# Banded attention divided behind the value product by transposed reciprocals, and a later place for some of VectorE's bit counts

## The chip, the cores and the metric

The kernel runs on one core of a Trainium2 chip. The metric is the device time of one execution in microseconds (us); lower is better. Engines are named as the profile names them: PE (TensorE, with PEld for its weight loads), DVE (VectorE), ACT (ScalarE), POOL (GpSimd), and SP, whose queue issues nearly all the DMAs.

## What is computed

The reference is one decoder block on 1024 tokens of width 1024. Two attention branches run side by side: a sparse one (branch a), in which an indexer scores all earlier keys and each query keeps its 256 best, and a banded one (branch b) with a window of 128 keys and a sink logit for each head. Each has 8 query heads and 2 key heads of width 64. Their outputs are gated, projected and added, and an MLP follows. The part that the change touches, cut:

```python
def swa_branch(q, k, v, sinks):                      # banded, branch b
    logits = einsum('bnqgrd,bnkgd->bngrqk', qb, kb) * HEAD_DIM ** -0.5
    logits = where(mask, logits, -inf)               # 0 <= t - s < 128
    p = softmax(concatenate([logits, sink], -1), -1)[..., :-1]
    return einsum('bngrqk,bnkgd->bnqgrd', p, vb)

def dsa_branch(q, k, v, q_idx, k_idx, w_idx, topk):  # sparse, branch a
    score = where(causal, einsum(relu(q_idx . k_idx), w_idx), -inf)
    _, sel = top_k(score, 256)                       # per query
    p = softmax(q . k[sel] * HEAD_DIM ** -0.5)       # not-yet-valid keys: -inf
    return p . v[sel]
```

## The kernel before

One launch goes through these stages, by the profile's clock: norm and first projections, indexer scores (up to about 240 us), the banded branch (240 to 440), the sparse branch (440 to 650), branch and output products (to 835), MLP up (to 1115) and MLP down (to the end). Float32 products run as three products of high and low halves.

**Steps and parts.** Each attention branch is a list of 16 steps, one for a pair (g, b): key head g with its four query heads, and query block b of 128 tokens. `pipeline` walks the list. The banded branch takes b = 0 to 7 for g = 0, then for g = 1; the sparse one takes the pairs in the order of `A_STEPS`, short ones first. In this text steps are numbered 0 to 15 (banded) and 16 to 31 (sparse). A step has two parts of two heads. A part's `scores` issues score products into a PSUM bank (L837), the masked minimum (L853, DVE), the exponential with its row sums (L856, ACT) and the reciprocals of the row sums (L860, DVE). The probabilities are then multiplied by the reciprocals: in the banded branch by L868 on DVE (`NORM` has 'd'), 128 x 256 for a head, in the sparse branch by L864 on POOL ('p'). `apply`, three parts later (`DEPTH` is 2), transposes the probabilities on PE (L879), splits them into halves (L104 on ACT, L109 on DVE, tile `of_w<-pt`), multiplies by the values (L884, L885, tile `pv`), and after the second part copies `pv` to SBUF (L892, ACT) and stores it.

**Bits.** The sparse branch's selection finds each query's 256th best score bit by bit. Query blocks 5 to 7 are counted on DVE: a bit is three counts (L676, 128 x 768, 896 and 1024) and some operations on 128 x 3 (L738, L739, and L737 on POOL), each bit waiting for the one before. Blocks 2 to 4 are counted on ACT (L678, with L741, L742 and L744 on DVE). `BITS` says how many DVE bits follow each banded step ('b') and precede each sparse step ('a'); there are 31 bits and a call that makes the thresholds. `select` (L776 to L782) then makes the mask of a block, on DVE and POOL.

**Filling work.** `fill` puts the gate products (tile `gt`, 128 x 512, 48 matmuls for a half gate) after steps, by `FILL`; the projections of later queries (tile `mm`) are spread likewise. The program is handed to a scheduler, which sets each engine's order from the program's order and its own timeline, so that an instruction may come well ahead of its place in the text. Each engine then runs its list strictly in order.

Of the kernel before, what the change touches and what calls it, by code (L numbers as in the profile page):

```python
# [16 lines left out]
ALU = mybir.AluOpType  # L17

P = 128
# [7 lines left out]
R = NH // NG  # L27
# [22 lines left out]
IB_BANK = ('tr', 'S', 'pt')  # L50
START = {'dve': 11, 'act': 11}
A_STEPS = [(0, 1), (0, 0), (0, 3), (0, 2), (1, 1), (1, 0), (1, 3), (1, 2), (1, 5), (1, 4), (1, 7), (1, 6), (0, 6), (0, 7), (0, 5), (0, 4)]
BITS = {'b': '2121212121212121', 'a': '1111112'}
ORDER = [(5, 0), (4, 0), (6, 0), (7, 0), (3, 0), (2, 0), (7, 1), (6, 1), (5, 1), (4, 1), (3, 1), (2, 1)]
GBUFS = 3
WBUFS = (2, 4)
# [11 lines left out]
EVAC = 'a'  # L68
# [26 lines left out]
def decoder_block(tc, I, out):  # L95
    nc = tc.nc
# [124 lines left out]
    ident = kept(P)  # L221
# [355 lines left out]
    for b in range(NB):  # L577
        ps = bank(IB_BANK[b % len(IB_BANK)], [P, 512], "mm")
        project(ps[:, :328], w, b)
        ik, st, sqk, ikr = (x() for x in small)  # L580
# [38 lines left out]
    u, o = {}, 0  # L619
# [47 lines left out]
    top, o = {}, 0  # L667
# [151 lines left out]
    def attention_parts(st):  # L819
# [9 lines left out]
        def scores(j0):  # L829
            if j0 == 0:  # L830
                st.mx, st.sm = att["mx"](), att["sm"]()
            both = bank("S", [P, 2, 2 * P], "S") if PAIR and N <= 2 * P else None

            def products(j, c, e):
                pS = both[:, j - j0] if both is not None else bank("S", [P, 512], "S")
                for a in range(2):
                    marks["S"] = nc.tensor.matmul(pS[:, :e - c], lhsT=st.unit(b, j), rhs=kT[:, a, k0 + c:k0 + e], start=a == 0, stop=a == 1).ins  # L837
                return pS

            if sink:  # L840
                with tc.issue_after(turned_i[0]):
                    nc.gpsimd.tensor_copy(st.both.rearrange("p (j n) -> p j n", j=2)[:, :, 0], sk[:, j0:j0 + 2])
            if both is not None:
                pS2 = [products(j, 0, N) for j in range(j0, j0 + 2)]
            for j in range(j0, j0 + 2):
                pe = st.both[:, (j - j0) * st.width:(j - j0 + 1) * st.width]
                p = pe[:, 1:] if sink else pe
                last = sk[:, j:j + 1] if sink else -MASKED
                for c in range(0, N, 512):
                    e = min(N, c + 512)  # L850
                    pS = pS2[j - j0] if both is not None else products(j, c, e)
                    init, last = last, st.mx[:, j, c // 512:c // 512 + 1]
                    nc.vector.tensor_tensor_reduce(out=p[:, c:e], in0=pS[:, :e - c], in1=st.bias(c, e), scale=-SCALE, scalar=init,  # L853
                                                   op0=ALU.add, op1=ALU.min, accum_out=last)
                pe = pe[:, :N + sink]
                nc.scalar.activation(pe, pe, AF.Exp, bias=last, scale=-1.0, accum_out=st.sm[:, j:j + 1])  # L856
                prob[j] = p
            on = NORM[st.name]
            inv = st.sm[:, j0:j0 + 2]
            nc.vector.reciprocal(inv, inv)  # L860
            for j in range(j0, j0 + 2):
                q, r = prob[j][:, :N], st.sm[:, j:j + 1]
                if on[j] == "p":
                    nc.gpsimd.tensor_scalar(q, q, r, 0.0, op0=ALU.mult, op1=ALU.add)  # L864
                elif on[j] == "a":
                    nc.scalar.activation(q, q, AF.Copy, scale=r)
                else:
                    nc.vector.tensor_scalar(q, q, r, None, op0=ALU.mult)  # L868

        def apply(j0):  # L870
            if j0 == 0:
                st.pv = bank("pv", [P, R, P], "pv")
            pv = st.pv[:, j0:j0 + 2]
            for a in range(0, n, 2):
                m = min(2, n - a)
                pt = bank("pt", [P, 2, 2, P], "pt")
                for k in range(m):
                    for j in range(2):
                        nc.tensor.transpose(pt[:, k, j], prob[j0 + j][:, (a + k) * P:(a + k + 1) * P], ident)  # L879
                ph, pl = att["ph"](), att["pl"]()  # L880
                split(ph[:, :m], pl[:, :m], pt[:, :m], "act")
                for k in range(m):
                    vs = v[:, kb0 + a + k].rearrange("p a d -> p (a d)")
                    nc.tensor.matmul(pv, lhsT=vs, rhs=ph[:, k], start=a + k == 0, stop=False)  # L884
                    st.last = nc.tensor.matmul(pv, lhsT=vs, rhs=pl[:, k], start=False, stop=a + k == n - 1).ins  # L885
            if j0 == 0:
                return

            o = att["o"]()
            marks["pv"] = st.last  # L890
            if EVAC == "a":
                nc.scalar.copy(o, st.pv)  # L892
            else:
                nc.vector.tensor_copy(o, st.pv)
            for x in range(2):
                stores.append(nc.sync.dma_start(st.dst[x, R * g:R * g + R, :, st.b * P:(st.b + 1) * P].rearrange("j d q -> d j q"), o[x * HD:(x + 1) * HD]).ins)
# [165 lines left out]
    for half in (1, 0):  # L1062
        for ft in range(KT):
# [12 lines left out]
            tr = bank("tr", [P, 4, P], "trx")  # L1076
# [351 lines left out]
```

## Time and profile before

| | us |
|---|---|
| median of 3 runs (lowest, highest) | 1456.59 (1454.28, 1456.62) |
| time of the profiled execution | 1455.47 |
| its span | 1453.7 |

| engine | busy us | share of the span |
|---|---|---|
| PE | 1374.5 | 95% |
| DVE | 1080.2 | 74% |
| ACT | 779.0 | 54% |
| POOL | 461.4 | 32% |

The shares are means over stages with different limits, and a busy PE is not PE at its peak. The change lies in the two attention branches, 410 of the 1453.7 us. So the rows further down are by stretch: A (240 to 380 us, banded steps 0 to 9), B (380 to 440, the other banded steps), C (440 to 510, sparse steps 16 to 20), D (510 to 560, steps 21 to 24) and E (560 to 650, the rest).

### The profile page before, as it was taken

The page shows a single profiled execution, that of the slowest core. Times are in us where ns is not written, and L with a number is a line of the kernel's source. Part 1 is how long each engine was busy: PE and PEld are TensorE (multiplying, and loading weights), DVE is VectorE, ACT ScalarE, POOL GpSimd, SP SyncE. Part 2 cuts the span into 40 slices and gives each one's busy share as a digit, 9 for nine tenths or more (in the row PEclk, how much of TensorE's full clock was granted, in tenths as well). Part 3 has the DMA queues.
Part 4 walks back from the last instruction along what each step waited for, and adds up shares of the span by engine and source line. Part 5 has one row for each costly group of instructions (what it writes and reads, how often), then busy time and mean ns, then how long its engine had stood idle before and what let it go on. Part 6 is the DMA issues. An engine that isn't in the chain of part 4 may idle for free.

```text
span 1453.7 us, 21243 instructions
## 1 busy us (share of the span) xinstructions
PE 1374.5 (95%) x7096; PEld 1163.6 (80%) x7096; DVE 1080.2 (74%) x2115; ACT 779.0 (54%) x1612; POOL 461.4 (32%) x455
## 2 busy tenths in 40 slices
PE   8999997888898899789999999999999999999998
PEld 6989886677797788677878778888888888888887
DVE  8667799999889988776753586566664788687674
ACT  6335445666783547654445476555554545445453
POOL 4373865663758773323515310000000000001001
PEclk9999998999999999899999999999999999999999
DMA  7321231322433221456456465344443978643323
GB/s 267 111 74 48 79 108 58 88 76 57 108 84 88 53 71 29 116 165 207 153 166 174 131 212 204 141 150 149 159 146 110 333 251 310 211 119 93 109 74 116
DMA packets 135822, 196.10 MB, mean 135 GB/s; under 512 B 16032, under 2 KB 59168, under 8 KB 135584
## 3 DMA queue, kind: packets, MB, share of 16 engines
q1 hardware_dynamic: 135568, 194.74, 42.6%
q8 instruction: 56, 0.92, 0.3%
q14 instruction: 54, 0.44, 0.1%
q10 hardware_dynamic: 144, 0.00, 0.0%
HBM read 132.03 MB, written 55.84 MB: 129 GB/s over the span
## 4 chain that ended last, share of the span: by engine, by line
PE 62%; DVE 21%; DMA 5%; ACT 4%; issue 4%; POOL 3%; SPq 1%; DVEq 0%; ACTq 0%; POOLq 0%
PE pu L1121 7%; PE pu L1123 7%; PE pu L1122 7%; DVE of_a L676 7%; PE pdx L1320 4%; PE pdx L1318 4%; PE pdx L1319 4%; PE pdy L1320 3%; PE pdy L1318 3%; PE pdy L1319 3%; DVE wide L853 2%; PE pso L113 2%; PE pso L115 2%; PE pso L114 2%; DMA uall<-z_d 2%
## 5 line engine op out<-in xcount | busy, mean ns | idle before, releaser
L1265 POOL TENSOR_TENSOR y<-x,gf 128x512 f32<-128x512 f32 x4 | 6.3, 1601 | 492.9 <-DVE x L1249 491.5
L104 ACT ACTIVATE dao<-da 128x512 fp32r<-128x512 f32 x112 | 70.0, 630 | 132.1 <-PE pdx L1320 52.5
L856 ACT ACTIVATE wide<-wide,of_a 128x257 f32<-128x257 f32 (+9 forms) x128 | 81.0, 634 | 80.4 <-DVE of_a L853 79.4
L113 PE MATMUL mm<-of_h,of_w 128*128 128x256 f32 x416 | 119.6, 288 | 0.5 <-ACT of_g L292 0.5
L114 PE MATMUL mm<-of_h,of_w 128*128 128x256 f32 x416 | 118.9, 287 | 0.0
L115 PE MATMUL mm<-of_h,of_w 128*128 128x256 f32 x416 | 118.7, 287 | 0.1
L676 DVE TENSOR_SCALAR_CACHE_REDUCE of_a<-wide,of_a 128x768 bf16<-128x768 bf16 (+5 forms) x93 | 106.1, 1141 | 1.0
L109 DVE TENSOR_TENSOR dao<-da,dao 128x512 fp32r<-128x512 f32 x112 | 76.4, 686 | 36.8 <-ACT dao L104 36.6
L1121 PE MATMUL pu<-XT,uo 128*128 128x512 f32 x256 | 99.8, 390 | 0.8 <-ACT snap L1154 0.8
L1122 PE MATMUL pu<-XT,uo 128*128 128x512 f32 x256 | 99.6, 389 | 0.0
L1123 PE MATMUL pu<-XT,uo 128*128 128x512 f32 x256 | 99.5, 389 | 0.0
L113 PE MATMUL gt<-of_h 128*128 128x512 f32 x224 | 91.4, 408 | 6.6 <-ACT of_h L335 6.6
L1319 PE MATMUL pdx<-dbo,dao 128*128 128x512 f32 x248 | 94.9, 389 | 0.0
L1318 PE MATMUL pdx<-dbo,dao 128*128 128x512 f32 x248 | 94.8, 390 | 0.0
L115 PE MATMUL gt<-of_h 128*128 128x512 f32 x224 | 91.0, 408 | 2.5 <-POOL of_h L109 2.5
L1320 PE MATMUL pdx<-dbo,dao 128*128 128x512 f32 x248 | 93.0, 390 | 0.0
L678 ACT ACTIVATE of_a<-uall,of_a 128x384 int8<-128x384 f32 (+2 forms) x93 | 66.8, 719 | 48.7 <-DVE of_a L744 28.5
L114 PE MATMUL gt<-of_h 128*128 128x512 f32 x224 | 90.8, 405 | 0.5 <-DVE of_h L336 0.5
L837 PE MATMUL S<-of_w 128*128 128x256 f32 (+3 forms) x320 | 79.4, 342 | 11.9 <-DVE of_a L853 11.9
L879 PE MATMUL pt<-kept,wide 128*128 128x128 f32 x408 | 72.7, 283 | 14.0 <-DVE of_a L739 6.3
L113 PEld LDWEIGHTS mm<-of_h,of_w 128*128 128x128 f32 x416 | 80.5, 194 | 1.6 <-ACT of_g L292 0.7
L115 PEld LDWEIGHTS mm<-of_h,of_w 128*128 128x128 f32 x416 | 80.1, 193 | 1.4 <-POOL of_w L109 0.5
(284 smaller groups left out, 4315.0 us busy)
## 6 DMA issues: line engine op xcount, KB each, us to landing
u_d<-u SPq DMA_DIRECT2D x112, 256.0 KB, 2.2
da<-u_d SPq DMA_DIRECT2D x112, 256.0 KB, 2.9
ur<-in_w_up_dram SPq DMA_DIRECT2D x32, 512.0 KB, 4.9
dr<-in_w_down_dram SPq DMA_DIRECT2D x64, 256.0 KB, 5.3
z_d<-of_g SPq DMA_DIRECT2D x32, 256.0 KB, 2.2
uall<-z_d SPq DMA_DIRECT2D x32, 256.0 KB, 3.4
raw<-in_w_out_dram SPq DMA_DIRECT2D x32, 256.0 KB, 4.2
of_g<-in_w_g_dram SPq DMA_DIRECT2D x28, 256.0 KB, 2.8
```

Source lines behind the costliest of these rows:

```text
L113: ins = nc.tensor.matmul(ps, lhsT=ah, rhs=bh, start=first, stop=False)
L114: nc.tensor.matmul(ps, lhsT=ah, rhs=bl, start=False, stop=False)
L115: nc.tensor.matmul(ps, lhsT=al, rhs=bh, start=False, stop=last)
L676: nc.vector.tensor_scalar(j, src, c, None, op0=ALU.is_lt, op1=ALU.add, accum_out=a)
L837: marks["S"] = nc.tensor.matmul(pS[:, :e - c], lhsT=st.unit(b, j), rhs=kT[:, a, k0 + c:k0 + e], start=a == 0, stop=a == 1).ins
L856: nc.scalar.activation(pe, pe, AF.Exp, bias=last, scale=-1.0, accum_out=st.sm[:, j:j + 1])
L1121: nc.tensor.matmul(ps, lhsT=ah, rhs=xh[:, at], start=f0, stop=False, skip_group_check=True)
L1122: nc.tensor.matmul(ps, lhsT=ah, rhs=xl[:, at], start=False, stop=False, skip_group_check=True)
L1123: nc.tensor.matmul(ps, lhsT=al, rhs=xh[:, at], start=False, stop=last, skip_group_check=True)
L1318: nc.tensor.matmul(ps, lhsT=ah[:, js], rhs=x[0][:, at], start=first, stop=False, skip_group_check=True)
L1319: nc.tensor.matmul(ps, lhsT=ah[:, js], rhs=x[1][:, at], start=False, stop=False, skip_group_check=True)
L1320: nc.tensor.matmul(ps, lhsT=al[:, js], rhs=x[0][:, at], start=False, stop=end, skip_group_check=True)
```

## The change

In the banded branch the probabilities are no longer multiplied by the reciprocals. After the value product of a step, its four columns of reciprocals are each spread over 128 columns and transposed on PE into one PSUM bank (`rb`, tag `tr`), so that row sums stand along the columns as in `pv`; ACT copies `pv` to SBUF as before, and DVE multiplies that copy by `rb` in place, ahead of the store. The sparse branch's own scaling on POOL stays. The second edit changes the table `BITS`: 20 instead of 24 calls after banded steps, and up to two ahead of each sparse step (calls past the thresholds do nothing).

```diff
-BITS = {'b': '2121212121212121', 'a': '1111112'}
+BITS = {'b': '1211121112111211', 'a': '2222222'}
...
             nc.vector.reciprocal(inv, inv)
-            for j in range(j0, j0 + 2):
+            for j in range(j0, j0 + 2) if st.name == "a" else ():
                 q, r = prob[j][:, :N], st.sm[:, j:j + 1]
...
             o = att["o"]()
             marks["pv"] = st.last
-            if EVAC == "a":
+            if st.name == "b":
+
+                rb = bank("tr", [P, R, P], "rb")
+                for j in range(R):
+                    nc.tensor.transpose(rb[:, j], st.sm[:, j:j + 1].to_broadcast([P, P]), ident)
+                nc.scalar.copy(o, st.pv)
+                nc.vector.tensor_tensor(o, o, rb, ALU.mult)
+            elif EVAC == "a":
                 nc.scalar.copy(o, st.pv)
```

In the changed file the transposes are L895, the copy L896 and the new product L897.

What the scheduler makes of it, at three places. First DVE in banded step 8, before:

```order
L860 RECIPROCAL of_a<-of_a 128x2
L676 TENSOR_SCALAR of_a<-wide,of_a 128x896
L744 TENSOR_SCALAR of_a<-of_a 128x3
L868 TENSOR_SCALAR wide<-wide,of_a 128x128 x2
L676 TENSOR_SCALAR of_a<-wide,of_a 128x1024
L738 TENSOR_TENSOR of_a<-of_a 128x3
```

and after (L741, L742 and L744 belong to ACT's bits):

```order
L741 TENSOR_TENSOR of_a<-of_a 128x3
L676 TENSOR_SCALAR of_a<-wide,of_a 128x1024
L742 SCALAR_TENSOR_TENSOR of_a<-of_a 128x3
L897 TENSOR_TENSOR of_a<-of_a,rb 128x512
L738 TENSOR_TENSOR of_a<-of_a 128x3
L744 TENSOR_SCALAR of_a<-of_a 128x3
L860 RECIPROCAL of_a<-of_a 128x2
```

The four L868 of a step are gone, and one L897 stands between the counts.

Second, DVE ahead of the 42nd pair of reciprocals, in sparse step 20. Before (L763 to L765 make the thresholds, L776 begins the mask of block 5):

```order
L738 TENSOR_TENSOR of_a<-of_a 128x3
L109 TENSOR_TENSOR of_w<-pt,of_w 128x256
L853 ISA wide,of_a<-S,of_a 128x256
L853 ISA of_a 128x1
L739 SCALAR_TENSOR_TENSOR of_a<-of_a 128x3
L763 TENSOR_SCALAR of_a<-of_a 128x3
L764 TENSOR_TENSOR of_a<-of_a 128x3
L853 ISA wide,of_a<-S,of_a 128x128
L853 ISA of_a 128x1
L765 TENSOR_TENSOR of_a<-of_a 128x3
L860 RECIPROCAL of_a<-of_a 128x2
L776 TENSOR_SCALAR of_a<-uall,of_a 128x768
```

and after:

```order
L441 TENSOR_TENSOR of_a<-of_a 128x512
L853 ISA wide,of_a<-S,of_a 128x256
L853 ISA of_a 128x1
L109 TENSOR_TENSOR of_w<-pt,of_w 128x256
L739 SCALAR_TENSOR_TENSOR of_a<-of_a 128x3
L676 TENSOR_SCALAR of_a<-wide,of_a 128x768
L853 ISA wide,of_a<-S,of_a 128x256
L853 ISA of_a 128x1
L676 TENSOR_SCALAR of_a<-wide,of_a 128x896
L860 RECIPROCAL of_a<-of_a 128x2
```

Where the thresholds stood, counts stand now. In all, 26 bits stood in the banded branch or ahead of it and 5 in the sparse one; now it is 24 and 7.

Third, PE near the end of sparse step 24, the first step of block 5. Before:

```order
L884 MATMUL pv<-of_w 128x256
L885 MATMUL pv<-of_w 128x256
L879 MATMUL pt<-kept,wide 128x128 x4
L884 MATMUL pv<-of_w 128x256
L837 MATMUL S<-of_w 128x512 x2
L885 MATMUL pv<-of_w 128x256
```

and after:

```order
L879 MATMUL pt<-kept,wide 128x128 x6
L884 MATMUL pv<-of_w 128x256
L115 MATMUL gt<-of_h 128x512
L113 MATMUL gt<-of_h 128x512
L114 MATMUL gt<-of_h 128x512
L115 MATMUL gt<-of_h 128x512
L837 MATMUL S<-of_w 128x512 x2
L885 MATMUL pv<-of_w 128x256
```

Gate products now stand among the last products of the step. Counted over the lists, with a step's end at its last value product, steps 0 to 9 hold 207 gate products before and 167 after, steps 10 to 16 24 and 26, steps 17 to 23 168 and 149, and steps 24 to 31 34 and 91.

## Rows read from the trace of the kernel before

**Rows 1.** Busy time by stretch; columns stand in its first line.

```profile
core 0: us, PE busy (x) PEld busy (x) DVE busy (x) ACT busy (x) POOL busy (x), PEclk, DMA share, GB/s
240.00:380.00 140.00, 115.51 (x691) 99.02 (x690) 135.62 (x399) 92.22 (x253) 74.74 (x112) 0.95 0.28 76
380.00:440.00 60.00, 55.62 (x428) 52.25 (x426) 49.18 (x144) 52.43 (x148) 38.78 (x46) 1.00 0.42 101
440.00:510.00 70.00, 61.48 (x380) 52.40 (x379) 68.36 (x160) 30.38 (x78) 54.51 (x54) 1.00 0.26 67
510.00:560.00 50.00, 50.00 (x291) 43.16 (x290) 40.17 (x84) 26.09 (x53) 32.01 (x25) 1.00 0.22 59
560.00:650.00 90.00, 77.82 (x470) 66.15 (x469) 72.27 (x173) 58.16 (x112) 30.77 (x27) 0.92 0.40 112
```

**Rows 2.** Chain that ended last, shares of the stretch by line: A, B, C, D.

```profile
by line: DVE of_a L676 41.0%; DVE wide L853 8.9%; DVE wide L868 8.7%; DVE of_w L109 6.2%; issue 5.5%; ACT of_a L678 3.4%; DVE of_a L741 3.0%; DVE wide L708 2.9%; DVE of_a L742 2.5%; DVE of_a L738 2.0%; DVE wide L709 2.0%; PE gt L113 1.7%; P
...
by line: issue 13.6%; ACT of_a L678 11.2%; ACT wide L856 8.9%; DVE wide L868 7.0%; DMA of_a<-of_a 6.7%; SPq L439 5.0%; DVE wide L853 4.7%; POOL of_a L441 4.6%; DVE of_a L742 4.3%; DVE of_a L744 4.1%; ACT of_a L436 3.1%; DVE of_w L109 3.1%; 
...
by line: DVE of_a L676 22.2%; issue 11.0%; DVE wide L853 9.2%; DVE of_w L109 6.3%; DVE of_a L738 4.2%; POOL of_w L456 3.7%; DVE uall L782 3.7%; POOL uall L777 3.6%; DVE of_a L441 3.6%; DVE of_a L781 3.5%; DVE uall L779 3.0%; DMA of_a<-of_a 
...
by line: PE gt L115 17.9%; PE gt L113 17.6%; PE gt L114 17.5%; PE S L837 15.0%; PE pt L879 13.1%; PE pv L885 7.9%; PE pv L884 7.6%; DVE wide L853 1.4%; ACT of_w L104 1.2%; DVE of_w L109 1.1%; issue 0.3%
```

**Rows 3.** Line L868 alone, by stretch, A and B: stretch, length, DVE busy, clock, DMA.

```profile
240.00:380.00 140.00, 17.49 (x43) 0.95 0.28 76
380.00:440.00 60.00, 12.88 (x22) 1.00 0.42 101
```

**Rows 4.** Instructions in order of time: start us, length us, engine, line, operation, count.

```profile
361.35 0.61 DVE L868 TENSOR_SCALAR wide<-wide,of_a 128x256 f32<-128x256 f32 x2
...
342.27 1.65 DVE L868 TENSOR_SCALAR wide<-wide,of_a 128x256 f32<-128x256 f32 x2
...
341.17 2.60 POOL L441 TENSOR_TENSOR of_a<-of_a 128x512 f32<-128x512 f32 x2
```

**Rows 5.** L109, L742 and L892 by line: count, then ns min/median/max, first and last start.

```profile
L109 DVE TENSOR_TENSOR of_w<-pt,of_w x112: 403/682/692, 250.9 to 646.4; 128x512 fp32r<-128x512 f32 x92, 128x256 fp32r<-128x256 f32 x20
...
L742 DVE SCALAR_TENSOR_TENSOR of_a<-of_a x31: 152/164/1245, 221.4 to 438.6; 128x3 int32<-128x3 int32 x31
...
L892 ACT COPY of_a<-pv x32: 563/574/595, 263.0 to 649.6; 128x512 f32<-128x512 f32 x32
```

**Rows 6.** Line L676 alone, by stretch, A and C.

```profile
240.00:380.00 140.00, 68.88 (x120) 0.95 0.28 76
...
440.00:510.00 70.00, 19.50 (x36) 1.00 0.26 67
```

**Rows 7.** DVE groups, 240 to 440 us: busy us, mean ns | idle before, releaser.

```profile
L738 DVE TENSOR_TENSOR of_a<-of_a 128x3 f32<-128x3 f32 x20 | 4.4, 222 | 0.0
...
L739 DVE SCALAR_TENSOR_TENSOR of_a<-of_a 128x3 f32<-128x3 f32 x11 | 1.7, 157 | 0.2
```

**Rows 8.** PE: a run of transposes on the chain, and gate products in order of time.

```profile
537.53 0.98 PE pt L879 x9
...
509.08 0.39 PE L115 MATMUL gt<-of_h 128*128 128x512 f32 x1
509.31 0.39 PE L113 MATMUL gt<-of_h 128*128 128x512 f32 x1
```

**Rows 9.** What DVE waited for in stretch A: us in total, times, longest.

```profile
DVE of_a L741 <- ACT of_a L678: 3.5, 2, 2.1
```

## The prediction

> **What bounds the kernel now.** The profile's page says that PE is busy 95% of the span and DVE 74%, a mean over stages. So I cut the two attention branches into five stretches and read busy time in each [rows 1], then the chain of work that ended last in each [rows 2], then the lines that the change touches, and last who waited.
>
> In stretch A, DVE is busy 135.62 of 140 us, and the chain is made of DVE lines: the counts 41.0%, the scaling L868 8.7%, which is 12.2 us [rows 1, 2]. What DVE waited for there is 3.5 us [rows 9]. A is bound by DVE. In B three engines stand close together, PE at 55.62, ACT at 52.43 and DVE at 49.18 of 60 us, and the chain passes from one to the other; L868 has 7.0% of it, 4.2 us [rows 1, 2]. In C DVE is busy 68.36 of 70 us and the counts lead the chain again. In D PE is busy for all 50.00 us and gate products alone hold 53% of the chain (17.9, 17.6 and 17.5), while DVE has 9.8 us free. In E no engine is full; PE has 12.2 us free [rows 1, 2]. So DVE's time is worth its length in A and C, about half in B, nothing in D; PE's time is worth its length in D.
>
> **The scaling, in A.** L868 costs 17.49 us of DVE there, in 43 instructions [rows 3]. Undisturbed, two of them take 0.61 us; with POOL at work, two took 1.65 us and ended as POOL's instruction did, 341.17 + 2.60 [rows 4]. At 0.305 us each the 43 would be 13.1 us, so 4.4 us of the 17.49 are stretch. The new product L897 reads SBUF and PSUM and writes 128 x 512. No row shows it; the nearest is L109 on `of_w<-pt`, the same size with one operand in PSUM, at a median of 682 ns and at most 692 [rows 5]. Ten steps cost 6.8 us. DVE gains 10.7 us if the stretch goes with L868, and 6.3 if it lands on the next instruction that can be held: the small L742 went from 152 to 1245 ns [rows 5]. I take 9.
>
> The row shows DVE held until POOL's instruction ends. The Trainium skill says so in "SBUF — State Buffer", section "SBUF: two separate sides": the port pair that the two engines share is locked for a whole instruction, and a DVE instruction takes part if it runs in a two-port mode or has two SBUF inputs. By that rule L897, with one SBUF input, is never held, which agrees with the maximum of 692 ns.
>
> **The bits, in A.** The table moves four calls; in the scheduler's order two bits move, from 26 and 5 to 24 and 7. A bit in A is 68.88 us / 20 = 3.44 us for its three counts and their accumulator reads (six instructions, 120 / 6 = 20 bits) [rows 6], and 0.222 + 0.157 for two small operations [rows 7]: 3.82, so 7.6 us for two. DVE loses 9 + 7.6 = 16.6 us in A. PE covers that: it gains 40 transposes at 0.98 / 9 = 0.109 us, 4.4 us, and loses 40 gate products at 0.23 us, 9.2 us [rows 8]. ACT has the same copies as before. I take the whole: **-16.6**, between -17 and -8 (with the wait of the third rival below).
>
> **The new waits.** The four transposes wait for DVE's reciprocals in PE's list. Before, the transposes of the probabilities waited for L868, which stood behind the same reciprocals, so no wait is longer. The reciprocals must now be kept until then; there are three sets for a pipeline three parts deep. Bank `tr` is otherwise free in these branches until their end. L897 is new behind ACT's copy (574 ns [rows 5]): while DVE stands at it, the counts and the next L853 are queued behind, and PE and ACT behind those. The store leaves later by L897's 0.68 us, and its reader comes only in E. I price this at nothing in the forecast, since the scheduler put counts between, and give it a rival.
>
> **Stretch B.** L868's 4.2 us leave the chain; its 12.88 us of DVE [rows 3] become six L897 at 0.68, 4.1 us. PE, nearly full, gets 24 transposes, 2.6 us. Bounds: -8.8 if DVE's saving counts, and +3 if PE's extra counts with two more gate products. I take **-3**.
>
> **Stretch C.** Two more bits. DVE counts there at 19.50 / 6 = 3.25 us a bit [rows 6], a little less than in A; I keep 3.82 with the small operations. DVE is full, and the masks of blocks 5 to 7 wait for the bits: **+7.6**, between +2 (if the free 9.8 us of D take them) and +7.6.
>
> **Stretches D and E.** The scheduler moved gate products later: steps 24 to 31 hold 91 instead of 34. 57 at 0.23 us are 13.1 us of PE, placed where PE has no free time in D and 12.2 us in E. Bounds 0 and +13.1. The row of D speaks for the full price, that of E for nothing; the added products stand in steps 24 and 25, across the border. I take **+6**.
>
> **Sum.** -16.6 - 3 + 7.6 + 6 = -6.0. The profiled execution took 1455.47 us (span 1453.7 and 1.8 around it), so 1449.5; the median of the runs, 1456.59, is 1.1 above the profiled one: **1450.6**. Its own range, with half the bounds at once, is 1443 to 1457.
>
> **First rival: the sparse branch takes back more than the banded gives.** The mechanism is the displaced gate products. In A they filled time in which PE waited for DVE and cost nothing; behind D they stand in a list that is full. Its price is all of 13.1 us there, and +3 in B, where step 16 now holds 24 of them and before none: -16.6 + 3 + 7.6 + 13.1 = +7.1, so 1463.7. It decides once gates and transposes cost 9.0 us together (16.6 - 7.6). For it: D's 50.00 of 50 and the 53% of gate products on the chain. Against it: DVE will be the later engine in C and D by two bits, and PE's wait for the masks is just what the scheduler fills.
>
> **Second rival: all is covered.** The gates go into E's 12.2 us and PE's waits for the masks, the bits into D's free DVE time: -16.6 - 4 + 2 + 0 = -18.6, so 1438. For it: two engines that are each full in only one of the two stretches. Against it: lists run in order, and no instruction moves up at run time.
>
> **Third rival: the swap gives DVE nothing.** L897 waits for the copy, which in ACT's list often stands behind exponentials and counts. At 0.9 us each in ten steps, about one and a half times the copy's 574 ns, the 9 us are gone, and the sum is -7.6 - 3 + 7.6 + 6 = +3, so 1459.6. For it: DVE has little slack and an ordered list. Against it: ACT is busy 92.22 of 140 us in A.
>
> A rule of the skill points the same way. "VectorE: DVE Perf Modes", section "The perf-mode tier table", has float32 tensor_scalar from SBUF at two elements a cycle, and tensor_tensor or any operand in PSUM at one. By the page's table of cycles a removed 128 x 256 would be an estimated 194 ns and L897 658 ns, so the 64 and 16 instructions would weigh 11.9 and 10.5 us, and the swap would save some 1.4 us in both branches. The rows have 30.4 us for the 64, undisturbed ones at 305 ns, so the measurement decides.
>
> **How the numbers follow.** Forecast 0.5, first rival 0.2, second 0.15, third 0.15. What can be told from no change is 0.2%, 2.9 us, so faster is below 1453.7 and slower above 1459.5. The forecast's own range puts 0.37 of its 0.5 on faster, 0.12 on the same and 0.01 on slower; the first rival 0.03 on the same and 0.17 on slower; the second 0.15 on faster; the third 0.03, 0.08 and 0.04. Sums: faster 0.55, same 0.23, slower 0.22. The range runs from the second rival's time to the first's, 1438 to 1463, and leaves out some 0.18 on both sides.
>
> **What would show it.** In the changed profile the copy of step 9 (the tenth L896; L892 before) should come some 17 us earlier; DVE should stay over 95% busy until then; L897 should be near 0.68 us each with no stretch, and the idle time ahead of it under 3 us in all. The first mask of block 5 (L776) should come some 12 us earlier than before, 20 from the banded branch less 7.6. Between it and the end of the sparse branch 6 us should be lost, with PE full and gate products on the chain up to step 25. The forecast is wrong in A if L742 and its like stretch by what L868 did, or if DVE waits ahead of L897; wrong behind it if the end of step 25 lies as far behind L776 as before, or 13 us further.

## The result, and the profile after

| | before | after |
|---|---|---|
| median us (lowest, highest; runs) | 1456.61 (1454.28, 1456.75; 4) | 1464.05 (1461.48, 1465.59; 4) |
| time of the profiled execution, its span | 1455.47, 1453.7 | 1461.48, 1459.5 |

The ratio is 1.0053 with an interval of [1.0037, 1.0068]: the change makes the kernel slower by half a per cent. The forecast had the wrong sign, and the time lies 1 us outside its range; it is within 0.4 us of the first rival's.

The rows from here on are those of the profiled executions, which lie 6.0 us apart where the medians lie 7.4. For the comparison the stretches are cut at ACT's copies of `pv`, so that both kernels have done the same steps at each cut: steps 0 to 9, 10 to 15, 16 and 17, 18 to 23, 24 and 25, 26 to 31. The kernel before:

```profile
core 0: us, PE busy (x) PEld busy (x) DVE busy (x) ACT busy (x) POOL busy (x), PEclk, DMA share, GB/s
240.00:380.20 140.20, 115.71 (x693) 99.22 (x692) 135.82 (x400) 92.42 (x255) 74.94 (x112) 0.95 0.28 76
380.20:434.90 54.70, 50.31 (x384) 47.03 (x384) 45.81 (x131) 47.44 (x135) 33.56 (x39) 1.00 0.41 99
434.90:445.80 10.90, 10.90 (x80) 10.20 (x80) 8.69 (x27) 7.20 (x19) 10.31 (x11) 1.00 0.55 121
445.80:537.60 91.80, 83.28 (x493) 70.89 (x492) 88.40 (x189) 38.87 (x96) 75.00 (x66) 1.00 0.23 62
537.60:562.60 25.00, 25.00 (x153) 21.06 (x151) 17.07 (x50) 17.03 (x34) 7.22 (x8) 1.00 0.18 49
562.60:649.60 87.00, 74.82 (x452) 64.16 (x452) 69.81 (x164) 55.92 (x109) 29.77 (x27) 0.92 0.41 115
```

and after, same steps, same columns:

```profile
240.00:371.50 131.50, 109.81 (x687) 96.86 (x686) 121.95 (x350) 91.32 (x251) 67.86 (x105) 0.95 0.27 73
371.50:419.90 48.40, 45.60 (x366) 43.22 (x364) 35.83 (x103) 43.80 (x121) 30.62 (x35) 1.00 0.44 111
419.90:442.00 22.10, 21.71 (x131) 19.03 (x132) 18.42 (x47) 12.05 (x34) 18.41 (x19) 1.00 0.35 87
442.00:532.30 90.30, 78.92 (x474) 66.83 (x474) 86.29 (x191) 39.17 (x95) 65.85 (x65) 1.00 0.24 62
532.30:568.30 36.00, 36.00 (x205) 30.80 (x204) 20.38 (x53) 17.82 (x36) 12.55 (x13) 1.00 0.17 52
568.30:655.70 87.40, 72.94 (x455) 60.34 (x454) 69.97 (x168) 56.68 (x108) 29.44 (x27) 0.98 0.39 115
```

By length: -8.7, -6.3, +11.2, -1.5, +11.0 and +0.4, +6.1 in all; what follows step 31 takes 804.1 and 803.8 us. The banded steps are 15 us shorter, and the next two steps and steps 24 and 25 give back 22.2. In those two places PE is busy for all or nearly all of the time (21.71 of 22.10, 36.00 of 36.00).

The gate products alone, by the same cuts, first before, then after (the second column is the length, then PE's busy time and the count):

```profile
240.00:380.20 140.20, 54.98 (x192) 35.85 (x192) 5.09 (x9) 0.95 0.28 76
380.20:434.90 54.70, 7.05 (x24) 4.12 (x24) 0.59 (x1) 1.00 0.41 99
434.90:445.80 10.90, 2.46 (x10) 1.81 (x10) 0.59 (x1) 1.00 0.55 121
...
537.60:562.60 25.00, 8.98 (x34) 6.10 (x34) 1.18 (x2) 1.00 0.18 49
```

```profile
240.00:371.50 131.50, 41.32 (x152) 26.72 (x152) 4.01 (x7) 0.95 0.27 73
371.50:419.90 48.40, 0.71 (x2) 0.30 (x2) 0.57 (x1) 1.00 0.44 111
419.90:442.00 22.10, 11.85 (x47) 8.54 (x48) 0.56 (x1) 1.00 0.35 87
...
532.30:568.30 36.00, 23.31 (x87) 15.35 (x87) 2.39 (x5) 1.00 0.17 52
```

The banded steps lost 62 products, at 0.23 us [rows 8] 14.3 us. Steps 16 and 17 got 37 more and steps 24 and 25 got 53 more, 20.7 us together, for 22.2 us of length; 27 of these 90 come not from the banded steps but from steps 18 to 23 (158 before, 131 after), which became only 1.5 us shorter. (The 0.23 us run from one product's start to the next. The busy times in the rows are higher, since they also count ends that overlap other work.) (A half gate is 24 such products, not 48 as the description of the kernel says.) The chain in steps 24 and 25 of after reads accordingly:

```profile
by line: PE gt L113 18.7%; PE gt L114 18.6%; PE gt L115 17.9%; PE S L837 11.6%; PE pt L879 10.7%; DVE wide L853 5.9%; PE pv L884 5.8%; PE pv L885 5.7%; POOL wide L864 3.2%; issue 3.1%; DVE of_w L109 0.7%; DVE of_a L860 0.5%; DVEq L109 0.1%;
```

More views of after. The transposes of reciprocals, with L897, in steps 0 to 9 and 10 to 15 (PE, PEld and DVE), and then four transposes in order of time with what follows them:

```profile
240.00:371.50 131.50, 7.91 (x40) 4.96 (x40) 6.11 (x9) 0.95 0.27 73
371.50:419.90 48.40, 4.48 (x24) 2.75 (x24) 4.09 (x6) 1.00 0.44 111
```

```profile
390.46 0.60 PE L895 MATMUL rb<-kept,of_a 128*128 128x128 f32 x4
390.90 0.60 PE L879 MATMUL pt<-kept,wide 128*128 128x128 f32 x4
```

The four are recorded as 0.60 us long, but the next product starts 0.44 us after the first, 0.11 us for each.

What DVE waited for in steps 0 to 9, which answers to [rows 9], and then L897 over the whole kernel, with its durations (ns, shortest, median, longest) and what DVE sat idle for ahead of it:

```profile
DVE of_a L860 <- ACT wide L856: 4.0, 3, 1.9
DVE of_a L741 <- ACT of_a L678: 2.7, 3, 1.5
DVE of_a L739 <- DVE of_a L742: 0.4, 1, 0.4
```

```profile
L897 DVE TENSOR_TENSOR of_a<-of_a,rb x16: 665/680/689, 261.9 to 422.2; 128x512 f32<-128x512 f32 x16
...
  ACT of_a L896: 0.3, 1
  DMA of_a<-of_a: 0.2, 1
```

Small operations of DVE in steps 0 to 9 (busy us, mean ns | idle before), first before, then after:

```profile
L741 DVE TENSOR_TENSOR of_a<-of_a 128x3 int32<-128x3 f32 x18 | 5.7, 315 | 3.5 <-ACT of_a L678 3.5
L742 DVE SCALAR_TENSOR_TENSOR of_a<-of_a 128x3 int32<-128x3 int32 x18 | 5.1, 283 | 0.0
L744 DVE TENSOR_SCALAR of_a<-of_a 128x3 int32<-128x3 int32 x18 | 4.3, 237 | 0.0
```

```profile
L738 DVE TENSOR_TENSOR of_a<-of_a 128x3 f32<-128x3 f32 x18 | 5.9, 326 | 0.1
L742 DVE SCALAR_TENSOR_TENSOR of_a<-of_a 128x3 int32<-128x3 int32 x17 | 5.7, 337 | 0.1
L741 DVE TENSOR_TENSOR of_a<-of_a 128x3 int32<-128x3 f32 x17 | 4.3, 253 | 2.7 <-ACT of_a L678 2.7
L744 DVE TENSOR_SCALAR of_a<-of_a 128x3 int32<-128x3 int32 x17 | 2.8, 164 | 0.1
L739 DVE SCALAR_TENSOR_TENSOR of_a<-of_a 128x3 f32<-128x3 f32 x9 | 2.4, 267 | 0.7 <-DVE of_a L742 0.4
```

### The profile page after: what moved, and what is told of

It reads as the page before. It is cut to its first block, busy times and chain, and to the rows that moved or that the text cites. A ratio compares the mean times of both kernels' runs of the same rounds, so it can differ in the third digit from the quotient of the medians.

```text
span 1459.5 us, 21272 instructions
## 1 busy us (share of the span) xinstructions
PE 1379.6 (95%) x7160; PEld 1168.3 (80%) x7160; DVE 1066.2 (73%) x2067; ACT 782.1 (54%) x1612; POOL 457.0 (31%) x455
## 3 DMA queue, kind: packets, MB, share of 16 engines
q1 hardware_dynamic: 135568, 194.74, 41.9%
## 4 chain that ended last, share of the span: by engine, by line
PE 65%; DVE 19%; DMA 4%; ACT 4%; issue 4%; POOL 2%; SPq 1%; DVEq 0%; ACTq 0%; POOLq 0%
PE pu L1130 7%; PE pu L1128 7%; PE pu L1129 7%; DVE of_a L676 6%; PE pdx L1327 4%; PE pdx L1325 4%; PE pdx L1326 4%; PE pdy L1327 3%; PE pdy L1325 3%; PE pdy L1326 3%; DVE wide L853 2%; PE pso L113 2%; PE pso L114 2%; PE pso L115 2%; PE gt L114 2%
## 5 line engine op out<-in xcount | busy, mean ns | idle before, releaser
L109 DVE TENSOR_TENSOR dao<-da,dao 128x512 fp32r<-128x512 f32 x112 | 76.4, 689 | 42.7 <-ACT dao L104 42.6
L676 DVE TENSOR_SCALAR_CACHE_REDUCE of_a<-wide,of_a 128x768 bf16<-128x768 bf16 (+5 forms) x93 | 106.2, 1142 | 1.2
L113 PEld LDWEIGHTS mm<-of_h,of_w 128*128 128x128 f32 x416 | 81.4, 196 | 1.3 <-DVE of_a L853 0.5
L114 PEld LDWEIGHTS mm<-of_h,of_w 128*128 128x128 f32 x416 | 81.5, 196 | 1.0
L115 PEld LDWEIGHTS mm<-of_h,of_w 128*128 128x128 f32 x416 | 81.2, 196 | 1.4 <-POOL of_w L109 0.5
```

The costliest lines, as they stand in the source:

```text
L113: ins = nc.tensor.matmul(ps, lhsT=ah, rhs=bh, start=first, stop=False)
L114: nc.tensor.matmul(ps, lhsT=ah, rhs=bl, start=False, stop=False)
L115: nc.tensor.matmul(ps, lhsT=al, rhs=bh, start=False, stop=last)
L676: nc.vector.tensor_scalar(j, src, c, None, op0=ALU.is_lt, op1=ALU.add, accum_out=a)
```

## The experiments

The theories. **Filling** (later: PE's account): the scheduler, finding less DVE work in the banded branch, puts less filling PE work there; it comes due where PE is full, at its full length. **Bits**: the two counts that moved cost more in the sparse branch than they bring. **New wait**: DVE's reciprocals now stop its list behind ACT's exponentials.

### One part of the change at a time

The swap alone has the changed file with `BITS` as before; the bits alone have the file before with the new table.

```diff
-BITS = {'b': '1211121112111211', 'a': '2222222'}
+BITS = {'b': '2121212121212121', 'a': '1111112'}
```

> The swap alone: division behind the value product by transposed reciprocals as in the changed kernel, the bits of both branches as in the kernel before. Three theories. Filling: the scheduler puts less filling TensorE work (gate products, 0.231 us each, and projections, 0.12 us) into the banded steps where VectorE has less to do; by the kernel's own order 93.8 us of it lie in steps 0 to 15 here, 104.9 in the kernel before and 89.5 in the changed one, so the loss stays for the most part although no bit has moved: 1458 to 1460 us, and steps 16 and 17 take some 18 us against 10.9 before. Bits: it is the two bits in the sparse branch that cost; without them the gain of the banded steps stands and the time is about 1447 us. New wait: VectorE's reciprocals and the bits behind them wait for ScalarE's exponentials in the banded steps, 5 us of new idle time, with the bits back in place: 1458 to 1464 us, with steps 16 and 17 as long as before.

Measured: 1469.63 us, ratio 1.0087 [1.0073, 1.0101], slower than the whole change. Some of that is not of this place: what follows step 31 takes 810.4 us against 804.1, and 4.4 us of it is one wait of PE in the MLP,

```profile
PE pdy L1325 <- ACT dao L104: 4.4, 1, 4.4
```

which no theory had. Up to step 31 the swap costs 7.8 us. Step 15 ends 5.6 us earlier than before, steps 16 and 17 take 28.3 us, steps 24 and 25 take 39.1 with 100 gate products (34 before):

```profile
429.30:457.60 28.30, 24.80 (x153) 21.69 (x153) 25.29 (x60) 14.25 (x40) 20.82 (x19) 0.98 0.25 59
...
534.00:573.00 39.00, 38.61 (x214) 32.90 (x213) 20.65 (x52) 18.07 (x36) 16.83 (x16) 1.00 0.16 48
```

So without any moved bit the loss is there, in the places that filling names; it doesn't need the bits. Nor does it need the reciprocals' wait, which is 0.3 us in steps 0 to 9 here (DVE's idle time there is 3.7 us more than before, ahead of other lines).

> The bits alone: the kernel before with the changed kernel's table of bits (two fewer 128x256 bits of VectorE in the banded steps 0 to 9, two more in the sparse steps), the division as before, with the broadcast multiply. Filling: the order keeps 103.4 us of filling TensorE work in steps 0 to 15 (104.9 before), so little is lost: about 1457 us, within 0.2% of the kernel before. Bits: what the sparse branch pays is here without the swap's gain: about 1463 us. New wait: no new wait is here, about 1457 us.

Measured: 1459.84 us, ratio 1.0021 [1.0008, 1.0035]: a small loss, between the two expectations. The banded steps gain 3.8 us, steps 24 and 25 lose 5.0 (51 gate products in place of 34, 3.9 us). Steps 16 and 17 become 8.0 us longer and steps 18 to 23 4.6 us shorter. Here it is projections (tile `mm`) that moved, 94 in steps 16 and 17 in place of 52, and DVE, too, is busy for 18.18 of the 18.90 us, so this run can't tell the bits' own price from that of the filling work.

### The displacement alone

```diff
+            n = 2 * self.ft + half
...
-                mm3(ps, wh, wl, h, l, kt == 0, kt == KT - 1)
+                with tc.issue_after(marks["hold"]) if n >= 21 and "hold" in marks else nullcontext():
+                    mm3(ps, wh, wl, h, l, kt == 0, kt == KT - 1)
```

`marks["hold"]` is the first sparse score product.

> The kernel before, with nothing of the change but its displacement of filling work: the gate halves from the 22nd on may be issued only behind the first sparse score product. By the order 154 gate products then stand in steps 0 to 9 and none in steps 10 to 15 (192 and 24 before; 152 and 2 in the changed kernel), and 90.5 us of filling TensorE work in all in steps 0 to 15 (104.9 and 89.5). Filling: the loss of the changed kernel appears without its gain, the banded steps end little earlier since they were not TensorE's: 1466 to 1470 us at the full price of the 14 us moved, 1460 at a half. Bits and new wait: nothing that they name is changed, about 1457 us.

Measured: 1474.51 us, ratio 1.0120 [1.0100, 1.0141], one of the two largest losses (the other is 1.0116 below), more than the full price. Rows of its steps 0 to 9 and 18 to 23:

```profile
240.00:382.00 142.00, 111.07 (x677) 95.84 (x676) 138.20 (x407) 93.22 (x256) 73.63 (x109) 0.93 0.28 74
...
457.40:554.50 97.10, 85.28 (x506) 73.42 (x505) 88.37 (x185) 39.76 (x97) 74.97 (x69) 0.98 0.24 63
```

Steps 0 to 9 don't get shorter with 36 fewer gate products in them (142.0 against 140.2 us): in the kernel before that work was free there. Steps 16 to 25 pay with 20.2 us (10.0, 5.3 and 4.9 by stretch), more than the 14 us that were moved. Up to step 25 PE's idle time rises by 15.6 us, about what was moved; the rest of the loss is mostly a lower clock (both in the table further down).

### The division left out

Seen from the changed file, with the table of bits of the kernel before:

```diff
-                rb = bank("tr", [P, R, P], "rb")
-                for j in range(R):
-                    nc.tensor.transpose(rb[:, j], st.sm[:, j:j + 1].to_broadcast([P, P]), ident)
                 nc.scalar.copy(o, st.pv)
-                nc.vector.tensor_tensor(o, o, rb, ALU.mult)
```

> Left out: the division of the banded branch, in either form (no multiply of the probabilities, no transposed reciprocals, no product behind). The bits are those of the kernel before. It is the bound of what any cheaper division can bring. By the prediction's own steps, in which VectorE's time is worth its length in steps 0 to 9 and half in 10 to 15, the 17.5 and the 4.2 us come back, less the 36 gate products, 8.3 us, that the order puts into steps 24 and 25 more than before: 1443 us, or 1435 were they free. TensorE's account (the runs so far: from step 0 to the end of step 25 TensorE's idle time is 37 us in the kernel before and 36 in the changed one, although VectorE lost 14 us of work in steps 0 to 9 alone; what moves the end of step 25 is TensorE's busy time): TensorE's work is that of the kernel before, so the end hardly moves: 1452 to 1458 us.

Measured: 1458.18 us, ratio 1.0011 [1.0001, 1.0021]. The prediction's own steps had given 1443 us; this is 0.2 us above the range of TensorE's account. With the whole division gone, 30.4 us of DVE by [rows 3], nothing is gained, although DVE's busy time in steps 0 to 15 falls by 22.3 us. Its six stretches:

```profile
240.00:375.60 135.60, 112.23 (x687) 96.14 (x686) 127.66 (x364) 92.72 (x255) 70.62 (x110) 0.96 0.27 73
375.60:425.20 49.60, 47.93 (x363) 45.07 (x362) 31.70 (x98) 43.69 (x123) 35.37 (x39) 1.00 0.45 114
425.20:443.80 18.60, 18.56 (x119) 16.33 (x118) 14.11 (x42) 12.74 (x36) 11.15 (x12) 1.00 0.36 86
443.80:534.50 90.70, 79.79 (x463) 70.20 (x463) 86.60 (x185) 38.56 (x94) 74.56 (x67) 0.92 0.24 62
534.50:569.40 34.90, 34.57 (x206) 30.03 (x205) 19.14 (x52) 19.62 (x39) 10.96 (x12) 1.00 0.16 46
569.40:652.00 82.60, 70.73 (x441) 60.35 (x440) 68.02 (x162) 54.72 (x105) 27.94 (x25) 0.96 0.41 122
```

Step 15 ends 9.7 us earlier. Steps 16 and 17 give 7.7 of that back, with 23 more gate products (5.3 us), and steps 24 and 25 another 9.9, with 36 more (8.3 us). Only 20 of these 59 products left the banded steps; steps 18 to 23 gave up 36 (122 in place of 158) and became only 1.1 us shorter. This is the shape of the changed kernel, without a new wait and without a moved bit. It bounds every cheaper division, as long as the filling goes where it went here.

### PE relieved

In both kernels one of the three products of the gates is left out:

```diff
-                mm3(ps, wh, wl, h, l, kt == 0, kt == KT - 1)
+                nc.tensor.matmul(ps, lhsT=wh, rhs=h, start=kt == 0, stop=False)
+                nc.tensor.matmul(ps, lhsT=wl, rhs=h, start=False, stop=kt == KT - 1)
```

> Left out: one of the three products of the gates' matmuls (high by low of the activations), a third of all gate products, in the kernel before. For the pair with the next run: by the order no gate product stands in steps 24 and 25 of either, and 33 and 112 in steps 18 to 23. TensorE has some 30 us less to do from 240 us on, so this one should be 15 to 30 us under the kernel before if TensorE's work counts there, and at most 8 us, what steps 24 and 25 held, if it is hidden behind VectorE.

> Left out: the same third of the gate products, in the changed kernel. TensorE's account and filling: with TensorE relieved the change does what VectorE's saving promises, at least 5 us less than the run before this one. Bits: what they cost in the sparse branch stays, 5 to 8 us more than the run before this one. New wait: nothing is gained in steps 0 to 9, 3 us more or less.

Measured: 1445.89 us (1444.91 to 1447.86) for the kernel before and 1438.03 us (1434.10 to 1439.84) for the changed one. Now the change is faster, by 7.9 us. Of the first run's two expectations neither came: it is 9.8 us under the kernel before as measured beside it (1455.66), far from the 15 to 30 of TensorE's account and just over the 8 of the other. The changed kernel gains some 25 us by the same relief (its ratio to the kernel before goes from 1.0053 to 0.9881). So before the change most of PE's relief brings nothing, and after it most of it counts. Steps 0 to 9 and 24 and 25, before and then after:

```profile
240.00:382.80 142.80, 119.15 (x697) 103.80 (x697) 140.56 (x391) 90.81 (x251) 75.93 (x114) 0.88 0.31 86
...
528.50:554.50 26.00, 19.72 (x110) 15.36 (x108) 24.21 (x57) 14.29 (x30) 13.59 (x10) 0.89 0.10 21
```

```profile
240.00:360.70 120.70, 104.56 (x685) 94.43 (x685) 117.53 (x332) 84.47 (x230) 71.40 (x110) 0.96 0.32 87
...
517.30:543.40 26.10, 20.08 (x118) 17.14 (x117) 26.04 (x59) 15.13 (x32) 11.56 (x9) 0.88 0.10 21
```

Steps 0 to 9 gain 22.1 us, and steps 24 and 25 lose nothing. Steps 16 to 23 take back 17.7 (89.6 and 107.3 us), since they hold two more bits and, by the order, 79 more gate products. With PE's load taken down the sign of the change turns; bits and new wait had forecast a loss or nothing. (The upper level of the clock is recorded as 0.95 in the first of the two, 1.00 in every other run; what follows step 31 takes 803.8 us in both, so its engines ran no slower there.)

### Attempts to keep the gain

Six versions of the changed kernel with another order or fewer transposes, each against a loss that its theory named.

```diff
-FILL = {'i': '000000000000', 'b': '0222011001010101', 'a': '1111011010101010'}
+FILL = {'i': '000000000111', 'b': '0332211010101010', 'a': '1100000000000000'}
...
+    with tc.issue_after(got[-1]) if got and (st.name, g, b) in AFTER else nullcontext():
```

(`got[-1]` is the gate half that `AFTER` names for the step whose score product this is.)

> The changed kernel, with the filling work held in the banded steps: another table of filling quotas, and the banded score products of steps 3 to 11 issued only behind a numbered gate half. By the order 221 gate products stand in steps 0 to 9, 29 in steps 10 to 15 and 51 in steps 16 and 17 (152, 2 and 46 in the changed kernel), and 101 us of filling TensorE work in steps 0 to 15 (89.5 there, 104.9 before). Filling: about 11 us of TensorE's work leave the full steps 16, 17, 24 and 25, and the banded steps cover it: about 1453 us. Bits and new wait: the cause is untouched, about 1464 us.

Measured: 1468.91 us, ratio 1.0081 [1.0066, 1.0095]; one of the six executions took 6436.8 us, which nothing here explains. Missed. Steps 24 and 25 fell to 20.5 us with 4 gate products, but steps 0 to 9 became 18.8 us longer than in the changed kernel for 17.6 us more of gate products (228 against 152). Forced ahead of score products, the filling costs its length there too: DVE then stands idle for 20.1 us in steps 0 to 9, and PE still for 24.9. Steps 16 and 17 take 47.9 us, steps 18 to 23 75.4.

```diff
-            inv = st.sm[:, j0:j0 + 2]
-            nc.vector.reciprocal(inv, inv)
+            if st.name == "a":
+                inv = st.sm[:, j0:j0 + 2]
+                nc.vector.reciprocal(inv, inv)
...
+                nc.vector.reciprocal(st.sm, st.sm)
                 rb = bank("tr", [P, R, P], "rb")
```

> The changed kernel with the banded branch's reciprocals taken at the end of a step, one 128x4 ahead of its transposes, in place of one 128x2 behind each part's exponentials: VectorE's list no longer stops behind ScalarE's exponentials. New wait: the 4.0 us that VectorE waited there in banded steps 0 to 9 go, 1459 us or better. Filling: by the order still fewer gate products stand in steps 0 to 9 (141, 192 before) and 84 in steps 24 and 25 and behind (91 in the changed kernel, 34 before), so 1462 to 1466 us. Bits: untouched, 1464 us.

Measured: 1471.16 us, ratio 1.0108 [1.0089, 1.0127], worse than both said. Step 9 ends 4.0 us earlier than in the changed kernel, and DVE waits 2.3 us for the exponentials where it waited 4.0. All of it and more is given back behind, in steps 18 to 23 (100.2 us) and 24 and 25 (37.4 us). So the wait was real, and taking a part of it away made step 9 end earlier but not the kernel faster.

```diff
-FILL = {'i': '000000000000', 'b': '0222011001010101', 'a': '1111011010101010'}
+FILL = {'i': '000000000000', 'b': '0222011001010101', 'a': '0000000000111111'}
```

> The changed kernel with another row of filling quotas for the sparse branch: none asked for by steps 16 to 25, the rest by steps 26 on, which lets the scheduler place them where its own timeline has room. The banded branch is as in the changed kernel (152 and 2 gate products in its two stretches), but 198 stand in steps 18 to 23 (127 there) and 53 in steps 24 and 25 (91 there, 34 before). Filling: 38 gate products of 0.231 us, 8.8 us, leave steps 24 and 25, where each cost its full length in the runs so far (12.2 us more of them made these steps 11 us longer in the changed kernel, 15.2 us 14 us longer in the swap alone), for steps in which TensorE waits for VectorE: 1455 us, 1459 if half of it is paid in steps 18 to 23. Bits and new wait: their causes are untouched, 1464 us.

Measured: 1461.17 us, ratio 1.0049 [1.0030, 1.0068], the same as the changed kernel. Steps 24 and 25 are 6.6 us shorter, steps 18 to 23 are 8.4 us longer, with 67 more gate products there. They don't hide behind DVE, which is busy 91.47 of 98.70 us. Part of it is the clock:

```profile
480.00:484.00 4.00, 2.32 (x15) 2.10 (x15) 4.00 (x11) 1.53 (x6) 3.74 (x6) 0.89 0.36 75
484.00:488.00 4.00, 2.91 (x12) 2.43 (x12) 3.96 (x14) 2.83 (x9) 1.52 (x4) 0.50 0.39 131
488.00:492.00 4.00, 4.00 (x15) 3.52 (x15) 3.94 (x15) 2.91 (x8) 3.04 (x5) 0.50 0.00 0
```

```diff
-            for j in range(j0, j0 + 2) if st.name == "a" else ():
+            for j in range(j0, j0 + 2) if st.name == "a" or g else ():
...
-            if st.name == "b":
+            if st.name == "b" and not g:
```

> The changed kernel with the swap in the first eight banded steps alone; steps 8 to 15 multiply the probabilities on VectorE as before, and the 32 transposes of reciprocals of these steps are gone (0.19 us each in the changed kernel). 160 and 35 gate products stand in the two stretches of the banded branch, 28 in steps 16 and 17, 55 in steps 24 and 25 (152, 2, 46 and 91 in the changed kernel; 192, 24, 10 and 34 before). Filling: 36 products, 8.3 us, leave steps 24 and 25, and 6 us of transposes leave the steps in which TensorE is the fullest: 1455 us. New wait: VectorE's waits lie in the first steps and stay, 1460 to 1464 us. Bits: 1464 us.

Measured: 1462.52 us, ratio 1.0056 [1.0037, 1.0074]. Missed. Steps 24 and 25 are 6.5 us shorter than in the changed kernel, as filling said, but steps 10 to 15 now take 59.8 us, more than in either kernel (48.4 and 54.7), with 42 gate products where the changed kernel has 2.

> Both of the last two: the swap in steps 0 to 7 alone, and the other row of quotas for the sparse branch. 160, 35, 18, 173 and 32 gate products stand in steps 0 to 9, 10 to 15, 16 and 17, 18 to 23, and from 24 on (152, 2, 46, 127 and 91 in the changed kernel; 192, 24, 10, 158 and 34 before). Filling: steps 24 and 25 hold no more than before, so what the swap and the bits gain in the banded steps is kept but for the bits' price in the sparse branch: 1450 us, 6 us under the kernel before. Bits: 1464 us. New wait: 1460 to 1464 us.

Both edits together. Measured: 1471.30 us, ratio 1.0116 [1.0098, 1.0135], far from the 1450 of filling. Steps 24 and 25 hold 32 gate products and take 27.9 us; but steps 10 to 15 take 60.1 us and steps 18 to 23 take 97.2 (48.4 and 90.3 in the changed kernel).

```diff
-                for j in range(R):
+                for j in range(2):
...
-                nc.vector.tensor_tensor(o, o, rb, ALU.mult)
+                nc.vector.tensor_tensor(o.rearrange("p (a b) d -> p a b d", a=2), o.rearrange("p (a b) d -> p a b d", a=2), rb[:, None].to_broadcast([P, 2, 2, P]), ALU.mult)
```

> Changed: the changed kernel with two transposes of reciprocals per banded step in place of four, so that heads 2 and 3 are divided by the row sums of heads 0 and 1. VectorE's product keeps its size. 32 transposes at 0.19 us, 6.2 us of TensorE, are gone; by the order 147, 7, 24, 200 and 40 gate products stand in steps 0 to 9, 10 to 15, 16 and 17, 18 to 23 and from 24 on (152, 2, 46, 127 and 91 in the changed kernel). TensorE's account: about 6 us less, 1458 us. Bits and new wait: as the changed kernel, 1464 us.

Measured: 1466.18 us, ratio 1.0069 [1.0057, 1.0081], no better than the changed kernel. Missed: steps 18 to 23 take 108.0 us with 200 gate products (131 in the changed kernel). (The 0.19 us for a transpose is busy time with its overlapping end; from start to next start a transpose takes 0.11 us, so the 32 left out free about 3 us and not 6.2. The same holds for the half swap.)

Behind step 31 the late reciprocals, the half swap, both edits and the two transposes lose another 2.6, 2.8, 5.6 and 5.1 us against the kernel before, which no theory names.

Filling had forecast 1450 to 1455 us for four of the six, and none came under the kernel before. So it says where the time of a given order goes; what another order will cost it didn't forecast.

### What the runs have in common

From step 0 to the end of step 25, PE's time is split here in three: busy time at full clock, busy time lost to a low clock (over slices of 2 us, busy time by one less the granted clock), and idle time. In the row "before, PE relieved" the level recorded as 0.95 counts as full.

| kernel | us to the end of step 25 | work | low clock | idle |
|---|---|---|---|---|
| before | 322.6 | 278.9 | 6.3 | 37.4 |
| after | 328.3 | 285.5 | 6.6 | 36.2 |
| swap alone | 333.0 | 282.3 | 13.4 | 37.3 |
| bits alone | 327.2 | 277.7 | 12.6 | 37.0 |
| no division | 329.4 | 282.4 | 10.6 | 36.3 |
| half and quotas | 337.5 | 284.4 | 14.1 | 39.0 |
| late reciprocals | 334.6 | 285.5 | 9.8 | 39.3 |
| two transposes | 334.4 | 282.6 | 14.4 | 37.4 |
| quotas | 328.7 | 282.1 | 13.8 | 32.8 |
| swap half | 333.0 | 280.9 | 11.0 | 41.1 |
| gates forced early | 340.2 | 285.0 | 11.7 | 43.6 |
| gates held back | 344.4 | 279.6 | 11.7 | 53.0 |
| before, PE relieved | 314.5 | 247.5 | 16.3 | 50.7 |
| after, PE relieved | 303.4 | 246.9 | 14.6 | 41.9 |

PE's idle time up to there is 36 to 39 us in eight of the twelve kernels with the full gates, whatever DVE has to do. In the changed kernel it fell by 1.2 us, while DVE's busy time fell by 24 us in steps 0 to 15 (181.6 to 157.8). So with the full gates, what the change did to the time up to step 25 is what it did to PE: 6.6 us more work, about what the 64 transposes hold PE for (6.0 us, from each one's start to the next product's). With PE relieved the change lowers the idle time by 8.8 us, from 50.7 to 41.9, and there DVE's saving shows. The same rows say which engine binds: in the kernel before, 31.4 us less work bring 8.1 us, since idle time and low clock take back 23.3; in the changed kernel 38.6 us less bring 24.9. The other orders also lose 3 to 8 us more to a low clock, which goes some way to say why none of them beats the kernel before: between steps 10 and 25 its clock is 1.00 in every stretch, as the rows above show, and so is that of after, while all ten others have dips there (0.92 in steps 18 to 23 of the run without division, 0.50 in the rows of the quota run).

## Why the prediction was wrong, step by step

**Stretch A.** Forecast -16.6, measured -8.7. DVE's busy time fell by 13.9 us (135.82 to 121.95). That is the lower end that the working gave, 6.3 + 7.6, in which the stretch that POOL gives lands on other instructions. In part it did: L738 went from 222 to 326 ns [rows 7], L739 from 157 to 267, L742 from a mean of 283 to 337. But L741 fell from 315 to 253 and L744 from 237 to 164; at their means before, the five lines would have taken 21.2 us and they took 23.8, so 2.6 of the 4.4 us show there. The bits were sized rightly (their counts fell from 68.88 to 62.05 us), and so was L897's 0.68 us. The longest L897 took 689 ns, so none was held by POOL, while L738, with two SBUF inputs, was (up to 1253 ns). The Trainium skill, "SBUF — State Buffer", section "SBUF: two separate sides", tells these two kinds of instructions apart in this way, and this trace agrees. The step that failed is "I price this at nothing": DVE's idle time rose by 5.2 us (4.4 to 9.6), 4.0 of it ahead of L860, behind ACT's exponentials.

**PE's part in A.** "PE covers that" held for A itself, and the transposes were priced rightly: from each one's start to the next product's, the 40 take 4.0 us (0.108 us in the median), against 4.4. The 7.91 us of busy time in the row above count each transpose's overlapping end too.

**Stretch B.** Forecast -3, measured -6.3, within its bounds. Only 2 gate products were left there, where 24 had stood; that lost cover reappears in steps 16 and 17.

**Stretch C.** Forecast +7.6. Steps 16 to 23 cost +9.7, but in another place: +11.2 in steps 16 and 17, where PE is full and got 37 more gate products, and -1.5 in steps 18 to 23, where the two bits lie and 27 gate products fewer. So the bits' own price isn't parted from the filling here. From step 17's end to the first L776 of block 5 it is 47.9 us against 43.3, which leaves them some 4.6, an estimate that puts all of the difference down to them. The view that the prediction named shows the sum: that L776 comes at 489.9 us against 489.0, not 12 us earlier. The working had priced displaced products behind step 23 alone; the 24 of step 16 stood only in the first rival.

**Stretches D and E.** Forecast +6, measured +11.4. The second step that failed is taking the displaced products at half their price. It is 5.4 us of the miss, beside 7.9 in A. It took both to turn the sign clearly: with this term alone put right the forecast's -6.0 would be -0.6, with A's alone +1.9. Steps 24 and 25 got 12.2 us more of gate products and became 11.0 us longer; the products fall due before E's free time comes.

**The sum.** Half the bounds at once give 1441.7 to 1461.5 us, not the 1443 to 1457 that the working states; the measured 1464.05 lies outside both.

**Why the first rival was right.** Its sum of +7.1 came out as +7.4 in the medians, and its mechanism, displaced filling at its full price, is what the runs show: the gates held back lose without the change, no division wins nothing, and with PE relieved the change wins. That the number fits so closely is luck, for its sizes were off against each other: A gave 8.7 and not 16.6, B gained 6.3 instead of losing 3, and the 9.7 of steps 16 to 23, for which it had the bits' 7.6, arose in steps 16 and 17 with 37 displaced products.

**What lay under it.** That DVE's time is worth its length in A, where it is busy 97%, was argued from A by itself. PE had 24.5 us idle there, and the scheduler used that room for work that is due later. When DVE's list got shorter the room did too (21.7 us), and a gain in A became a debt in D. The third rival, that the swap gives DVE nothing, had the wrong place: L897 waited 0.3 us for the copy, and DVE waited ahead of L860.

What stays open: the swap's 7.8 us up to step 31, the bits' 3.2 and the 6.1 of both don't add up, since each edit brings another order, and the experiments can't part an edit from its order. Whether some order holds 192 gate products in the shorter steps 0 to 9 at less than their length isn't known; the one that forced them there didn't. All eleven other kernels with the full gates have a higher median than the kernel before, even the bits alone, in which the division is untouched. So it isn't excluded that a part of each loss, and of the change's, is only that another order suits these steps less than the one before.

## What to carry to other kernels

Where a scheduler fills one engine's idle time in a stage that another engine binds, don't price that stage alone: follow the filling work to where it falls due, and charge it there at full length if that place is full. Add up the filled engine's work and idle time over all stages between which work can move, and ask which of the two the change lowers. Leaving the whole operation out is a cheap first test: here it gained nothing. But that bounds a cheaper form only while the filling goes where it went; with PE relieved the change did win.

## What was not expected of the hardware

The clock dips. In the quota run PE was idle for 1.68 and 1.09 us of two slices of 4 us (480 to 488 above), and the granted clock fell to 0.50, the level of 1.2 GHz. It stayed there until after 492, though PE was busy for all of the last 4 us. The gaps come ahead of the fall; if they are its cause, which no run shows apart, a gap can cost more than its length: the row 488 to 492 alone has 4 us of work at half the clock.

The time for which POOL holds DVE doesn't all go with the instruction that shows it: with L868 gone, some operations on 128x3 became longer (L738 by 104 ns and L742 by 54 ns on average) and others shorter (L741 by 62 and L744 by 73), 2.6 us more in all.
